# A step of the second layer's experts in another order: next gate products, this pair's outputs, next transposes, then the branch

## Chip, cores, metric

The kernel runs on one core of a Trainium2 chip. The metric is the device time of one execution, in microseconds; the number that counts is the median of three runs. The profile below is of one further execution, and its own time stands beside the median in the table.

## What is computed

Two layers of a backbone over 512 latent tokens of width 1024. Each layer is a mixer followed by a channel mixer of 32 experts; each token goes to two of them. All arithmetic that matters here is float32. The expert part of the reference, which both layers end with:

```python
def hier_moe(h, ...):                # h: 512 tokens x 1024
    ...                              # top-1 group of 4, then top-2 of its 8 experts
    for e in range(N_EXPERTS):       # 32
        he = (silu(t @ w_gate[e]) * (t @ w_up[e])) @ w_down[e]   # 1024 -> 256 -> 1024
        out = out + dense_w[:, e:e + 1] * he
x = x + g2 * hier_moe(h2, ...)
```

The kernel does not run each expert over all tokens: the routing sorts the tokens by expert, and an expert gets 64 slots (`SLOT`) at once. An expert with more than 64 tokens is run again for the rest, decided on the chip by counts.

## The kernel before

The change concerns `experts` in its second-layer form (`l == 1`, `sent = True`). The experts are taken in 16 pairs, `pair(j)` being the expert numbers `p` and `p + 16`, one pair a step. The functions of a step, with the lines under which the profile lists them:

- `windows(j)` (L493, L496): ScalarE copies the pair's 2 x 64 token columns out of the sorted tokens `m.xs` into `m.xT`. `window(m.xr, ...)` does the same into `m.xr` for the expert that may have a second 64 tokens.
- `gate_up` (L357): 16 float32 matmuls of TensorE (32 records in the trace, two for each) for gate and up of both experts into PSUM bank `pg` (`mps0`). The weights come in four tiles of 1 MB: two hold the input rows of `c` 0 to 3, one for each expert, and two those of `c` 4 to 7, so the first eight matmuls need the first two tiles and the last eight need all four.
- `act` (L362, L363): silu on ScalarE into `m.sg`, times up on VectorE into `m.h`.
- `turn` (L370, L371): two transposes of `m.h` on TensorE into bank `ph` (`mps1`), and ScalarE's copy of them to `m.hT`. In the kernel before, `m.hT` is the memory of `m.sg`, so there is one buffer for transposed rows.
- `down` (L430): 8 float32 matmuls (16 records) with two more 1 MB weight tiles, into banks `py` (`mps2`, `mps3`).
- `once` (L623, L614, L615): VectorE weights the two halves of `py` into `ys`, and GpSimd scatters them by an indirect DMA to `yd`, a table of rows in HBM.
- `more_of` (L451, L452, L453, L370, L371, L459, L631, L615): the whole chain again for one expert of the pair with up to 64 more tokens. It reads the pair's six weight tiles again, and uses `m.sg`, `m.h`, `m.hT` and bank `ph`.
- `first(j + 1, None)`: `gate_up`, `act`, `turn` of the next pair and `windows(j + 2)`.

Which of the two sides of a branch is run (the label `few{l}_{j}`, L669) is decided by the larger count of the pair: with 64 tokens or fewer `few` is run, otherwise the `Else` side, which is laid out directly behind the branch. Every engine that has work in either side branches for itself.

The order around it is that in which the code is written: the whole of `experts` stands in a manual schedule, and each engine runs its instructions in program order. What makes one engine wait for another are semaphores that the framework sets by data and buffers.

The weights are a stream of 96 tiles of 1 MB for the layer (`Stream.emit`, L322 for gate and up, L324 for down, all issued by SyncE). The pool `W` has 13 buffers free for it and one more lies under the tag `more`; 14 tiles are loaded ahead. After that `st.emit(6, j)`, written behind the branch of step `j`, issues the next six tiles into the six buffers of pair `j`, which `more_of` may read as long as the branch is not over. After the 16th pair, `summed` (L653, L657) reads `yd` back in four 1 MB loads and VectorE adds it to the residual `X`; the 16th pair itself goes through another way to `X`, and `done` (L1798) writes the output.

Of the kernel before, what the change touches and what calls it, by code (L numbers as in the profile page):

```python
# [8 lines left out]
F32 = mybir.dt.float32  # L9
# [8 lines left out]
P = 128  # L18
D = 1024
# [97 lines left out]
class Route:  # L117
# [9 lines left out]
    def tile(self, i):  # L127

        k, v, sm = self.k, self.k.nc.vector, self.k.small
        g, e = self.lg[:, i, 0:4], self.lg[:, i, 4:36]  # L130
        mx, er = self.mx, self.er
        r4 = k.rio[:, 28:32]
        t4 = sm.tile([P, 4], F32, name="t4", tag="rt4", bufs=2)
        gr = sm.tile([P, 1], F32, name="gr", tag="rgr", bufs=2)
        t = sm.tile([P, 32], F32, name="t32", tag="rt32", bufs=2)
        em = sm.tile([P, 32], F32, name="em", tag="rem", bufs=2)
        v.tensor_reduce(mx[:, 0, i:i + 1], g, axis=AX.X, op=OP.max)
        v.scalar_tensor_tensor(t4, g, mx[:, 0, i:i + 1], r4, op0=OP.is_ge, op1=OP.mult)
        v.tensor_reduce(gr, t4, axis=AX.X, op=OP.max)
        v.tensor_scalar(t4, r4, gr, -BIG, op0=OP.not_equal, op1=OP.mult)  # L140
        v.tensor_tensor(em.rearrange("p (g x) -> p g x", g=4), e.rearrange("p (g x) -> p g x", g=4),
                        t4[:, :, None].to_broadcast([P, 4, 8]), op=OP.add)
        for c in range(2):
            m, r = mx[:, 1 + c, i:i + 1], er[:, c, i:i + 1]
            v.tensor_reduce(m, em, axis=AX.X, op=OP.max)
            v.scalar_tensor_tensor(t, em, m, k.rio, op0=OP.is_ge, op1=OP.mult)
            v.tensor_reduce(r, t, axis=AX.X, op=OP.max)
            v.tensor_scalar(self.EL[:, c, i], k.rio, r, None, op0=OP.is_equal)
            if c == 0:
                v.scalar_tensor_tensor(em, self.EL[:, 0, i], -BIG, em, op0=OP.mult, op1=OP.add)  # L150
            v.tensor_scalar(self.EL[:, 2 + c, i], k.rio, r, None, op0=OP.is_lt)
        for q in range(2):
            v.tensor_tensor(self.Eb[:, i, 32 * q:32 * q + 32], self.EL[:, 2 * q, i], self.EL[:, 2 * q + 1, i], op=OP.add)
# [141 lines left out]
def pair(j):  # L295

    return 8 * (j % 2) + j // 2
# [55 lines left out]
def gate_up(k, m, st, p, cs):  # L353

    for c in cs:
        for h in range(2):
            k.nc.tensor.matmul(m.pg[64 * h:64 * h + 64, :], m.xT[:, c, 64 * h:64 * h + 64], st.gu(p, h, c), start=(c == 0), stop=(c == 7))  # L357


def act(k, m):  # L360

    k.nc.scalar.activation(m.sg, m.pg[:, 0:256], AF.Silu)  # L362
    k.nc.vector.tensor_tensor(m.h, m.sg, m.pg[:, 256:512], op=OP.mult)  # L363


def turn(k, m, n=P):

    nc = k.nc
    for f in range(2):
        nc.tensor.transpose(m.ph[:, f * P:f * P + n], m.h[0:n, f * P:(f + 1) * P], k.ident[0:n, 0:n])  # L370
    nc.scalar.copy(m.hT[:, :, 0:n], m.ph[:, 0:2 * P].rearrange("p (f s) -> p f s", f=2)[:, :, 0:n])  # L371
# [52 lines left out]
def down(k, m, st, p):  # L424

    nc = k.nc
    for n in range(2):
        for f in range(2):
            for h in range(2):
                nc.tensor.matmul(m.py[n][64 * h:64 * h + 64, :], m.hT[:, f, 64 * h:64 * h + 64],  # L430
                                 st.dn(p, h, f)[:, 512 * n:512 * n + 512], start=(f == 0), stop=(f == 1))
# [43 lines left out]
def experts(k, l, m, st, res, rt, h2d, X, ahead, done):  # L475
# [8 lines left out]
    def ahead_of(label, row, p, most, limit):  # L484

        c = nc.values_load(res.cnt[0:1, row, p:p + 1], engines=(PE,), min_val=0, max_val=most,
                           skip_runtime_bounds_check_because="counts of at most 512 tokens")
        tc.mark_branch_hint_location(label, hint=c > limit, engines=(PE,))

    def window(x, at, act=False):  # L490

        e = mybir.EngineType
        o = nc.values_load(at, engines=(e.Activation if act else e.DVE,), min_val=0, max_val=1024 - SLOT,  # L493
                           skip_runtime_bounds_check_because="starts of at most 960")
        for c in range(4):
            (nc.scalar.copy if act else nc.vector.tensor_copy)(x[:, 2 * c:2 * c + 2], m.xs[c][:, :, bass.ds(o, SLOT)])  # L496

    def windows(j):
        p = pair(j)
        for h in range(2):  # L500
            window(m.xT[:, :, 64 * h:64 * h + 64], res.start[0:1, 0, p + 16 * h:p + 16 * h + 1], True)
# [28 lines left out]
    sent = l == 1  # L530
# [69 lines left out]
    def outs():  # L600
        m.one = Outs(tile([P, 512], "oh"), [tile([P, D], f"y{i}") for i in range(2)])
        m.two = Outs(tile([P, 512], "C0"), [tile([P, D], "S")])
        m.tmp = k.work.tile([P, 512], F32, name="tmp", tag="C1")

    if sent:
        ys = [k.work.tile([P, D], F32, name="ys", tag=f"y{i}") for i in range(2)]
        yx = k.work.tile([P, D], F32, name="yx", tag="S")[:, 0:512]
    else:
        outs()

    def send(n, row, y):

        ix = k.small.tile([P, 1], I32, name="ix", tag="ix", bufs=3)
        nc.vector.tensor_copy(ix, row)  # L614
        nc.gpsimd.indirect_dma_start(out=k.yd[:, :] if n == D else k.yd.rearrange("r (h d) -> (r h) d", h=2), in_=y, in_offset=None,  # L615
                                     out_offset=bass.IndirectOffsetOnAxis(ap=ix, axis=0), bounds_check=1024 * (D // n) - 1, oob_is_err=False)

    def once(j, p):

        y = ys[j % 2]  # L620
        for n in range(2):
            c = slice(512 * n, 512 * n + 512)
            nc.vector.scalar_tensor_tensor(y[:, c], m.py[n], res.w0[:, p:p + 1], m.g2[:, c], op0=OP.mult, op1=OP.mult)  # L623
        send(D, res.tok0[:, p:p + 1], y)
# [9 lines left out]
    def first(j, due):  # L634

        ahead_of(f"few{l}_{j}", 0, pair(j), 512, SLOT)
        gate_up(k, m, st, pair(j), range(8))
        act(k, m)
        if due:
            due.add(k, m, X, (0, 1))  # L640
        turn(k, m)
        if j < 15:
            windows(j + 1)
        if due:
            due.add(k, m, X, (2, 3))
# [13 lines left out]
    for j in range(16):  # L659
        p = pair(j)  # L660
        last = j == 15
        window(m.xr, res.second[0:1, p:p + 1], True)
        ahead_of(f"few{l}_{j}", 0, p, 512, SLOT)
        if j:
            down(k, m, st, p)
        if sent and not last:
            once(j, p)
            few = tc.If(count(0, p, 512) <= SLOT, preferred_fallthrough_block=False, label=f"few{l}_{j}")
            with few as more:  # L669
                first(j + 1, None)  # L670
            with more.Else():
                ahead_of(f"both{l}_{j}", 3, p, 1, 0)
                with tc.If(count(2, p, 3) == 2) as other:
                    more_of(p, 1, res.w[:, 1, p + 16:p + 17], res.tok[:, 1, p + 16:p + 17])
                with other.Else():
                    more_of(p, 0, res.w[:, 1, p:p + 1], res.tok[:, 1, p:p + 1])
                both = tc.If(count(3, p, 1) <= 0, preferred_fallthrough_block=False, label=f"both{l}_{j}")
                with both as rest:
                    pass
                with rest.Else():  # L680
                    with tc.If(count(2, p, 3) == 3):
                        window(m.xr, res.start[0:1, 1, p + 16:p + 17])
                        more_of(p, 1, res.w[:, 1, p + 16:p + 17], res.tok[:, 1, p + 16:p + 17])
                    with tc.If(count(0, p, 512) > 2 * SLOT):
                        with tc.For_i(2, count(1, p, 8), 1) as r:
                            for h in range(2):
                                at = bass.ds(r * 32 + p + 16 * h, 1)
                                for b, t in ((m.ic[:, h:h + 1], res.start), (m.tw[:, h, 0:1], res.w), (m.tw[:, h, 1:2], res.tok)):
                                    nc.vector.tensor_copy(b, t.rearrange("p r e -> p (r e)")[:, at])
                            for h in range(2):  # L690
                                window(m.xr, m.ic[0:1, h:h + 1])
                                more_of(p, h, m.tw[:, h, 0:1], m.tw[:, h, 1:2])
                first(j + 1, None)
            st.emit(6, j)
            continue
        if sent:
            outs()
            summed()
        weighed(k, m, res.w0[:, p:p + 1], res.tok0[:, p:p + 1])
# [1178 lines left out]
```

## Time and profile before

| | us |
|---|---|
| median of three runs (1397.38 to 1403.32) | 1401.59 |
| the profiled execution | 1409.57 |
| span of its instructions | 1407.8 |
| TensorE busy in the span | 1214.5 (86%) |
| VectorE busy | 745.5 (53%) |
| ScalarE busy | 513.8 (36%) |
| mean DMA rate over the span | 242 GB/s |

The second layer's expert steps fill the last fifth, from about 1100 us to 1376 us; behind them is the end of the kernel. Times in all rows are microseconds from the start of the span. TensorE's records appear as PE, its weight loads as PEld, VectorE as DVE, ScalarE as ACT, GpSimd as POOL, SyncE as SP; a q behind an engine means its sequencer. "Idle before" is the engine's gap just ahead of an instruction, with what ended it; "issue" there means that the profile shows nothing that was waited for.

### The profile page before, as it was taken

How to read it: one execution, taken by the hardware profiler on the slowest of the kernel's cores; microseconds unless marked ns; L12 is line 12 of the kernel's file. 1: busy time of each engine (PE TensorE's matmuls, PEld its weight loads, DVE VectorE, ACT ScalarE, POOL GpSimd, SP SyncE). 2: the span in 40 equal slices, each digit the busy share in tenths (PEclk: the TensorE clock that was granted, in tenths of full speed). 3: DMA queues.
4: the chain of work that ended last, by engine and by line, in shares of the span. 5: the costliest groups of instructions: out<-in, count | busy, mean ns of one | idle time of the engine just before them, and what ended most of it. 6: DMA issues, size and time to landing. Idle time of an engine off the chain costs nothing. (4 is left out here: it accounts for less than half of the span.)

```text
span 1407.8 us, 19802 instructions
## 1 busy us (share of the span) xinstructions
PE 1214.5 (86%) x6894; PEld 788.7 (56%) x6894; DVE 745.5 (53%) x1599; ACT 513.8 (36%) x1235; POOL 288.4 (20%) x270
## 2 busy tenths in 40 slices
PE   4998778989987999989979999999995787777875
PEld 2788645445764444444468898997873343333332
DVE  2435788899567545655683455667246411111116
ACT  3444445476444423433351233345224311211111
POOL 0044346586012111111230002220002000000000
PEclk9999989899997999999989999999997999999998
DMA  9411123737656889989766354453367698888883
GB/s 368 157 60 34 74 106 129 297 132 260 268 219 210 328 356 405 421 318 406 327 200 222 117 203 150 147 184 127 144 239 269 244 372 346 344 349 347 326 358 128
DMA packets 59297, 341.11 MB, mean 242 GB/s; under 512 B 9817, under 2 KB 10073, under 8 KB 24370
## 3 DMA queue, kind: packets, MB, share of 16 engines
q1 hardware_dynamic: 50834, 314.68, 57.3%
q0 software_dynamic: 8224, 23.61, 5.1%
q8 instruction: 105, 1.72, 0.5%
q14 instruction: 134, 1.10, 0.2%
HBM read 321.96 MB, written 21.80 MB: 244 GB/s over the span
## 5 line engine op out<-in xcount | busy, mean ns | idle before, releaser
L357 PE MATMUL mps<-w,xT 128*64 128x512 f32 x1024 | 251.9, 643 | 41.5 <-issue 26.7
L357 PEld LDWEIGHTS mps<-w,xT 128*64 128x64 f32 x1024 | 101.9, 148 | 185.8 <-issue 180.9
L806 PE MATMUL ps_c<-wch,hxh 128*128 128x256 f32 x512 | 147.4, 288 | 2.0 <-ACT hxh L812 2.0
L808 PE MATMUL ps_c<-wch,hxl 128*128 128x256 f32 x512 | 145.8, 285 | 1.5 <-DVE rm_m L98 0.9
L807 PE MATMUL ps_c<-wcl,hxh 128*128 128x256 f32 x512 | 146.0, 285 | 0.0
L363 DVE TENSOR_TENSOR mix<-mix,mps 128x256 f32<-128x256 f32 x32 | 13.5, 421 | 234.3 <-ACT mix L362 234.3
L430 PE MATMUL mps<-w,mix 128*64 128x512 f32 x512 | 118.6, 605 | 8.1 <-ACT mix L371 7.2
L362 ACT ACTIVATE mix<-mps 128x256 f32<-128x256 f32 x32 | 12.3, 384 | 275.6 <-PE mps L357 272.8
L997 POOL TENSOR_TENSOR acc<-acc,ctp 128x497 f32<-128x497 f32 (+14 forms) x71 | 103.2, 1481 | 29.6 <-ACT ctp L996 29.6
L806 PEld LDWEIGHTS ps_c<-wch,hxh 128*128 128x128 f32 x512 | 98.9, 193 | 7.8 <-issue 4.2
L808 PEld LDWEIGHTS ps_c<-wch,hxl 128*128 128x128 f32 x512 | 98.8, 193 | 4.5 <-issue 1.7
L807 PEld LDWEIGHTS ps_c<-wcl,hxh 128*128 128x128 f32 x512 | 98.9, 193 | 4.2 <-issue 3.4
L411 POOL TENSOR_TENSOR X<-X,tmp 128x512 f32<-128x512 f32 x32 | 41.2, 1287 | 204.7 <-ACT tmp L410 181.4
L400 PE MATMUL mps<-oy,ooh 128*128 128x512 f32 x272 | 74.8, 416 | 1.9 <-ACTq L729 1.7
L430 PEld LDWEIGHTS mps<-w,mix 128*64 128x64 f32 x512 | 35.4, 138 | 72.5 <-issue 55.5
L413 DVE TENSOR_TENSOR X<-X,mps 128x512 f32<-128x512 f32 x101 | 64.6, 683 | 5.4 <-PE mps L400 4.3
L806 PE MATMUL ps_o<-woh,yTh 128*128 128x512 f32 x160 | 63.8, 401 | 2.9 <-DVE res L1541 1.7
L400 PEld LDWEIGHTS mps<-oy,ooh 128*128 128x128 f32 x272 | 49.9, 193 | 25.5 <-issue 11.7
L807 PE MATMUL ps_o<-wol,yTh 128*128 128x512 f32 x160 | 63.5, 397 | 0.0
L808 PE MATMUL ps_o<-woh,yTl 128*128 128x512 f32 x160 | 62.9, 394 | 0.0
L812 POOL TENSOR_TENSOR vs<-v,vs 128x512 fp32r<-128x512 f32 x16 | 23.0, 1440 | 182.1 <-ACT vs L812 174.7
L991 DVE SCALAR_TENSOR_TENSOR acc<-z,cl,acc 128x508 f32<-128x508 f32 (+14 forms) x49 | 58.9, 1225 | 0.0
(430 smaller groups left out, 2389.8 us busy)
## 6 DMA issues: line engine op xcount, KB each, us to landing
w<-in_w_gu_dram SPq DMA_DIRECT2D x128, 1024.0 KB
w<-in_w_down_dram SPq DMA_DIRECT2D x64, 1024.0 KB
wada<-in_w_ada_dram SPq DMA_DIRECT2D x48, 1024.0 KB
wc<-in_c_w_in_dram SPq DMA_DIRECT2D x16, 1024.0 KB
wo<-in_c_w_out_dram SPq DMA_DIRECT2D x8, 1024.0 KB
X<-in_x_dram SPq DMA_DIRECT2D x4, 1024.0 KB
wo<-in_ab_w_out_dram SPq DMA_DIRECT2D x4, 1024.0 KB
yd<-zero SPq DMA_DIRECT2D x4, 1024.0 KB
```

Of the source, the lines that this page charges most:

```text
L357: k.nc.tensor.matmul(m.pg[64 * h:64 * h + 64, :], m.xT[:, c, 64 * h:64 * h + 64], st.gu(p, h, c), start=(c == 0), stop=(c == 7))
L363: k.nc.vector.tensor_tensor(m.h, m.sg, m.pg[:, 256:512], op=OP.mult)
L400: k.nc.tensor.matmul(po, self.oh[:, i * P:i * P + P], y[:, 512 * n:512 * n + 512], start=start and y is self.y[0], stop=stop and y is self ...
L411: k.nc.gpsimd.tensor_tensor(X[i][:, c], X[i][:, c], m.tmp, op=OP.add)
L413: k.nc.vector.tensor_tensor(X[i][:, c], X[i][:, c], po, op=OP.add)
L430: nc.tensor.matmul(m.py[n][64 * h:64 * h + 64, :], m.hT[:, f, 64 * h:64 * h + 64], st.dn(p, h, f)[:, 512 * n:512 * n + 512], start=(f == 0 ...
L806: k.nc.tensor.matmul(out, lh, rh, start=start, stop=False)
L807: k.nc.tensor.matmul(out, lh, rl, start=False, stop=False)
L808: k.nc.tensor.matmul(out, ll, rh, start=False, stop=stop)
L812: for i in (k.nc.scalar.copy(hi, src), (eng or k.nc.vector).tensor_tensor(lo, src, hi.bitcast(F32), op=OP.subtract)):
L991: pin(nc.vector.scalar_tensor_tensor(d, zz, w, d, op0=OP.mult, op1=OP.add))
L997: nc.gpsimd.tensor_tensor(d, d, tp, op=OP.add)
```

## The change

For the second layer, steps 0 to 14 are written in a new order. Before: outputs of pair `j` (`down`), `once`, then the branch, in both sides of which the next pair's `first(j + 1)` stands. Now: gate and up of pair `j + 1`, `down` of pair `j`, `act` of `j + 1`, `windows(j + 2)`, `turn` of `j + 1`, `once` of `j`, and then the branch, whose `few` side is empty. So that the transposed rows of pair `j` outlive the gate products of pair `j + 1`, there are two buffers: `hTs[0]`, in unused columns of the tile `ys` of tag `S`, for `turn` and `down`, and `hTs[1]`, the old place, for `more_of`. `st.emit(6, j)` stays behind the branch. The first layer's order is the same as before.

```diff
     if sent:
-        yx = k.work.tile([P, D], F32, name="yx", tag="S")[:, 0:512]
+        yx = k.work.tile([P, D], F32, name="ys", tag="S")
+        hTs = [yx[:, 512:768].rearrange("p (f s) -> p f s", f=2), m.hT]
+        yx = yx[:, 0:512]
@@ in the loop over j
         ahead_of(f"few{l}_{j}", 0, p, 512, SLOT)
-        if j:
-            down(k, m, st, p)
         if sent and not last:
+            gate_up(k, m, st, pair(j + 1), range(8))
+            m.hT = hTs[0]
+            if j:
+                down(k, m, st, p)
+            act(k, m)
+            if j < 14:
+                windows(j + 2)
+            turn(k, m)
+            m.hT = hTs[1]
             once(j, p)
             few = tc.If(count(0, p, 512) <= SLOT, preferred_fallthrough_block=False, label=f"few{l}_{j}")
             with few as more:
-                first(j + 1, None)
+                pass
             with more.Else():
...
-                first(j + 1, None)
             st.emit(6, j)
             continue
         if sent:
+            m.hT = hTs[0]
+        if j:
+            down(k, m, st, p)
+        if sent:
+            m.hT = hTs[1]
             outs()
             summed()
```

Three places in the built program. First TensorE around branch 1, the second of the loop. In the kernel before, `few`'s side of branch 0 ends here with the gate products and transposes of pair 1 (L357 and the first L370), and then come `down` of pair 1 and branch 1 (L669):

```order
L357 MATMUL mps_15807<-w,xT 64x512 x16
L370 MATMUL mps_15808<-ct,mix 128x128 x2
L669 UNCONDITIONAL_BRANCH
L486 TENSOR_LOAD cnt
L488 REGISTER_ALU
L1874 BRANCH_PREFETCH_HINT
L430 MATMUL mps_15809<-w,mix 64x512 x4
L430 MATMUL mps_15810<-w,mix 64x512 x4
L479 TENSOR_LOAD cnt
L669 COMPARE_AND_BRANCH
```

In the changed kernel the same step, behind branch 0, has the gate products of pair 2, `down` of pair 1, the transposes of pair 2 and branch 1 (L680):

```order
L695 UNCONDITIONAL_BRANCH
L486 TENSOR_LOAD cnt
L488 REGISTER_ALU
L1889 BRANCH_PREFETCH_HINT
L357 MATMUL mps_15807<-w,xT 64x512 x16
L430 MATMUL mps_15809<-w,ys 64x512 x4
L430 MATMUL mps_15810<-w,ys 64x512 x4
L370 MATMUL mps_15808<-ct,mix 128x128 x2
L479 TENSOR_LOAD cnt
L680 COMPARE_AND_BRANCH
```

The gate products of pair 2 have moved from behind branch 1 to the place right behind branch 0, and the transposes from ahead of `down` to behind it.

Second, SyncE behind branch 0, where `st.emit(6, 0)` issues its six tiles (the numbers behind `w_` tell the tiles apart). In the kernel before:

```order
L678 UNCONDITIONAL_BRANCH
L684 UNCONDITIONAL_BRANCH
L669 UNCONDITIONAL_BRANCH x2
L322 DMA w_16574<-in_w_gu_dram 128x2048
L322 DMA w_16576<-in_w_gu_dram 128x2048
L324 DMA w_16578<-in_w_down_dram 128x2048
```

In the changed kernel the same tiles, under other numbers:

```order
L680 UNCONDITIONAL_BRANCH
L689 UNCONDITIONAL_BRANCH
L695 UNCONDITIONAL_BRANCH
L322 DMA w_16527<-in_w_gu_dram 128x2048
L322 DMA w_16529<-in_w_gu_dram 128x2048
L324 DMA w_16531<-in_w_down_dram 128x2048
```

Nothing moved on SyncE: the six issues stand behind branch 0 in both.

Third, where TensorE reads the first two of these tiles, among the gate products of pair 2, whose other two tiles (`w_15805`, `w_15895`) are the last of the 14 that are loaded ahead. In the kernel before this stands in both sides of branch 1 (L669):

```order
L357 MATMUL mps0_15807<-w_15805,xT_15815 64x512
L357 MATMUL mps0_15807<-w_15895,xT_15815 64x512
L357 MATMUL mps0_15807<-w_16574,xT_15815 64x512
L357 MATMUL mps0_15807<-w_16576,xT_15815 64x512
...
L370 MATMUL mps1_15808<-ct_68,mix_15816 128x128 x2
L669 UNCONDITIONAL_BRANCH
```

In the changed kernel it stands ahead of `down` of pair 1, whose weights are `w_15801` and `w_15803`:

```order
L1889 BRANCH_PREFETCH_HINT
L357 MATMUL mps0_15807<-w_15805,xT_15815 64x512
L357 MATMUL mps0_15807<-w_15895,xT_15815 64x512
...
L357 MATMUL mps0_15807<-w_16527,xT_15815 64x512
L357 MATMUL mps0_15807<-w_16529,xT_15815 64x512
...
L430 MATMUL mps2_15809<-w_15801,ys_16219 64x512
L430 MATMUL mps2_15809<-w_15803,ys_16219 64x512
```

The first read of the batch's tiles has moved from behind branch 1 to behind branch 0, with eight matmuls between branch and read.

## Rows read from the trace of the kernel before

**Rows 1.** Windows of the steps; busy us of PE, PEld, DVE, ACT, POOL, clock, DMA share, GB/s.
```profile
1109.66:1366.61 256.95, 200.53 (x913) 86.14 (x910) 38.16 (x76) 48.77 (x206) 18.58 (x19) 0.95 0.88 352
1126.92:1144.72 17.80, 13.33 (x52) 6.29 (x50) 1.99 (x4) 3.25 (x14) 0.97 (x1) 0.88 0.93 369
1144.72:1164.83 20.11, 17.09 (x89) 8.08 (x85) 2.50 (x6) 3.90 (x16) 0.97 (x1) 0.95 0.83 334
```
**Rows 2.** SyncE's waits from 1000 us on: who waited for what, us, times, longest.
```profile
SPq L322 <- PE mps L357: 119.6, 9, 14.7
SPq L322 <- PEq L678: 73.5, 5, 14.9
```
**Rows 3.** The engines' waits from 1095 us on, the same columns.
```profile
PE mps L357 <- issue: 20.4, 10, 2.9
...
PE mps L370 <- DVE mix L363: 15.6, 15, 1.1
...
PE mps L430 <- ACT mix L371: 7.2, 14, 0.7
PE mps L357 <- PEq L486: 7.1, 5, 2.3
```
**Rows 4.** Windows from two of SyncE's issues (rows 8) on, columns as in rows 1.
```profile
1144.72:1146.90 2.18, 2.18 (x7) 1.16 (x5) 0.00 (x0) 0.00 (x0) 0.00 (x0) 0.50 0.62 132
1146.90:1159.50 12.60, 11.07 (x62) 5.48 (x60) 1.98 (x4) 3.25 (x14) 0.74 (x1) 1.00 1.01 426
...
1164.83:1167.00 2.17, 1.05 (x6) 0.50 (x8) 1.57 (x3) 0.00 (x0) 0.26 (x1) 1.00 0.57 113
1167.00:1171.40 4.40, 4.40 (x24) 1.50 (x21) 0.00 (x0) 0.00 (x0) 0.73 (x1) 1.00 1.00 400
```
**Rows 5.** Timeline of TensorE, steps 2 to 4: start, us, instruction, count, idle before.
```profile
1136.53 3.65 PE L430 MATMUL mps<-w,mix 128*64 128x512 f32 x16 [0.46 <-ACT mix L371]
1143.12 8.88 PE L357 MATMUL mps<-w,xT 128*64 128x512 f32 x32 [2.94 <-issue]
1153.07 0.44 PE L370 MATMUL mps<-ct,mix 128*128 128x128 f32 x2 [1.07 <-DVE mix L363]
1153.97 3.65 PE L430 MATMUL mps<-w,mix 128*64 128x512 f32 x16 [0.46 <-ACT mix L371]
...
1165.95 7.09 PE L357 MATMUL mps<-w,xT 128*64 128x512 f32 x32 [1.25 <-PEq L486]
...
1175.09 3.65 PE L430 MATMUL mps<-w,mix 128*64 128x512 f32 x16 [0.63 <-ACT mix L371]
1180.88 8.88 PE L357 MATMUL mps<-w,xT 128*64 128x512 f32 x32 [2.13 <-issue]
```
**Rows 6.** Timeline from the last steps on, all engines.
```profile
1349.10 7.18 PE L357 MATMUL mps<-w,xT 128*64 128x512 f32 x32 [2.72 <-issue]
...
1358.25 3.65 PE L430 MATMUL mps<-w,mix 128*64 128x512 f32 x16 [0.46 <-ACT mix L371]
...
1363.04 0.97 POOL L615 DMA_INDIRECT yd<-ys,ix  x1 [14.55 <-DVE ix L614]
1364.58 9.39 PE L357 MATMUL mps<-w,xT 128*64 128x512 f32 x32 [2.68 <-issue]
1366.61 2.19 SPq L653 DMA_DIRECT2D yt<-yd  x4
...
1374.91 10.71 DVE L657 TENSOR_TENSOR X<-X,yt 128x512 f32<-128x512 f32 x16
```
**Rows 7.** Line 669, the branch, on TensorE's sequencer: ns min/median/max.
```profile
L669 PEldq COMPARE_BRANCH  x19: 87/481/5350, 1119.8 to 1358.8; - x19
```
**Rows 8.** Timeline of SyncE at one batch: start, from first to last issue, count.
```profile
1164.83 1.09 SPq L322 DMA_DIRECT2D w<-in_w_gu_dram  x2
```
**Rows 9.** Timeline of TensorE where the loop begins.
```profile
1107.70 9.64 PE L357 MATMUL mps<-w,xT 128*64 128x512 f32 x32 [3.73 <-ACT mix L496]
```
**Rows 10.** Timeline of ScalarE there.
```profile
1104.95 1.78 ACT L496 COPY xT<-xs 128x128 f32 x8
```

## The prediction

> **What bounds the kernel now.** Only the second layer's expert steps and what follows them are touched, so I read that stretch. First the windows cut at the moments when SyncE starts a batch of six weight tiles [rows 1]: 14 steps in 256.95 us, a step of 17.8 us where `few` is taken and 20.1 where the `Else` side is. Of steps 0 to 14, five (3, 5, 7, 9, 11) take the `Else` side: the waits count five for its line L678 [rows 2]. In a step TensorE is busy for 13.3 of 17.8 us and the DMAs for 0.93 of the time, so neither is full alone, and one must ask who waits for whom. TensorE's waits [rows 3] are the 15.6 us for the activation, 7.2 us for the copy of the transposes, and 27.5 us at the branch (20.4 + 7.1); no wait for a weight tile stands among them. SyncE in turn waits 193.1 us for TensorE (119.6 + 73.5) before it may refill buffers [rows 2]. So today TensorE's chain with its branch stalls sets the pace, and the weights arrive in time, with little to spare: a batch is 6.3 MB, at 426 GB/s [rows 4] 14.8 us, and 2.2 us pass first at 113 to 132 GB/s; together 17.0 of the 17.8 us.
>
> **What the order does to the weights.** There are buffers for 14 tiles, six for a pair. Batch j goes into the buffers of pair j and is issued when TensorE has left branch j, before and after the change: nothing moves on SyncE. Before, its first two tiles (`w_16574`, `w_16576`) are read behind `down`, activation and branch of the next step, about 17 us later. Now gate and up of pair j + 2 come directly behind branch j, and their last eight matmuls read exactly these two tiles (`w_16527`, `w_16529`). TensorE must now wait in the middle of each `gate_up` for tiles that could not be issued earlier. The wait closes a loop: batch issued, two tiles land, half a `gate_up`, activation, transposes, branch, buffers free, next batch issued. I cost one turn of it.
>
> Issue to landing of the second tile: in the 2.17 us behind an issue the DMAs start 0.25 MB, in the 4.40 us behind that 1.76 MB [rows 4]; 2.1 MB are under way after 6.8 us. The scatter of `once` (0.5 MB), issued at most 2 us earlier in the new order, shares the queue, 1.2 us at 400 GB/s. I take 8.0; ends 6.8 and 9.0 (a start-up twice as long).
>
> Second half of `gate_up`: half of 7.09 is 3.55. Behind idle times of 2 us and more `gate_up` took 8.88 instead of 7.09 [rows 5] since its first part ran at the lower of the two clocks, a granted 0.50 (1.2 of 2.4 GHz) in the window [rows 4]; all of the excess in one half makes 5.33. Another time it took 7.18 behind 2.72 idle [rows 6]. I take 4.6.
>
> By the Trainium skill (TensorE: Matmul & The Clock Gate, section HAM oscillation) a wait for a DMA in each tile makes each tile start at the lower clock. By that rule it would be 5.33 every time, rival C; the rows here show both.
>
> From the end of `gate_up` to the release of the buffers, `few` taken: from the start of `down` to the next `gate_up` it was 6.59, 5.79 and 6.33 us [rows 5, 6], of which up to 5.35 are the branch instruction itself [rows 7]; since `down` takes 3.65, TensorE's sequencer evidently starts on the branch soon after `down` begins. In the new order the transposes stand between, and wait 1.07 us for the activation [rows 5], which runs beside `down`; the branch starts that much later: 1.07 + 6.3 = 7.4 to the next `gate_up`. The release comes about 1 us ahead of it, as on the `Else` side today (issue at 1164.83, `gate_up` at 1165.95 [rows 5, 8]). So 6.4; ends 5.9 and 6.7. The 1.07 and 0.46 us that TensorE idles for activation and copy are thus gone from TensorE, but `down` then covers a part of the branch stall less.
>
> The same, `Else` taken: `down` to issue was 10.86 us (1153.97 to 1164.83); the transposes come on top (0.44), and the copy out of bank `mps1`, since `more_of` writes that bank (0.46 as for L430): 11.8; ends 11.3 and 12.3.
>
> With 0.1 for the hand-over a turn is 0.1 + 8.0 + 4.6 + 6.4 = 19.1 us (`few`) or 24.5 (`Else`), against 17.8 and 20.1 now. VectorE, ScalarE and GpSimd are busy under 4 us a turn [rows 1], the windows and the copy of ScalarE beside `down`, so none of them ends last.
>
> **The two ends of the loop.** Batch 0 was issued at 1109.66, 1.96 us after `gate_up` of pair 1 started at 1107.70 [rows 9]. Now that `gate_up` comes ahead of branch 0. It can start at about 1106, when ScalarE has copied half of its window [rows 10], ends 9.4 later, and the release follows 6.4 after that: batch 0 at 1121.8, 12.1 us later than before.
>
> From batch 0, thirteen turns (branches 1 to 13: 8 `few`, 5 `Else`) lead to batch 13: 8 x 19.1 + 5 x 24.5 = 275.3, so 1397.1. `gate_up` of pair 15 ends 12.7 later at 1409.8. Before it ended at 1373.97 [rows 6]: 35.8 us later.
>
> The read-back of `yd`: before, pair 14's `down` and scatter ran ahead of this `gate_up`, which hid them: the adds (L657) start 0.94 us behind its end. Now `down` of pair 14 comes behind it: 3.65, then 4.71 until the load is issued (1361.90 to 1366.61), then about 5 until 1 MB is there (8.0 less 2.5 for the second tile, less part of the scatter): the adds start 13.4 behind, 12.4 later than before. What follows is as before.
>
> **Sum.** 35.8 + 12.4 = 48.2 us. The profiled execution would go from 1409.57 to 1457.8. It lay 8.0 us above the median; on the median, 1401.59 + 48.2 = 1449.8, and I say 1449. With all low ends a turn is 16.4 or 21.8, under the 17.0 that the DMAs need for a batch; with 17.0 and 21.8 the sum is about 15 us more than now. With all high ends (21.1, 26.7) it is about 77 more. All terms will not lie at one end, so 1424 to 1475.
>
> **Rivals.**
> B, not slower: the weights do arrive in time, as they would if the pool had buffers free beyond the 14. Then only TensorE's chain counts: 9 `few` turns save 0.9 us (7.4 instead of 1.07 + 0.44 + 0.46 + 6.3), 5 `Else` turns 1.07, and the first `gate_up` starts 1.7 earlier: 15 us, less the 12.4 us at the read-back: 1399, no change. For it: no wait for a tile shows today. Against it: the built order, in which the tile is issued behind the branch and read half a `gate_up` later. It decides where `down` or `gate_up` waits for no tile. 0.06. If the branch stall shrinks too, 9 x 2 less: 1381, faster: 0.03.
>
> C, slower still: the second half runs at the lower clock each time, 13 x 0.73 = 9.5 us more: 1459. For it 8.88 in the rows, against it 7.18. 0.18.
>
> D, less slow: the empty `few` side makes the jump shorter, by one copy of `first`, and the branch no longer stalls. Then the release waits only for the transposes, 4.1 + 0.3 behind `gate_up`: 2.0 x 9 less, 1431. Against it: the `few` jump still passes four copies of `more_of`. 0.10.
> By the Trainium skill (Runtime: NRT & Kernel Launch, section Instruction fetch mechanics) a taken branch stalls if its target is outside the pages that the sequencer holds. The 5.35 us here agree with that; how many pages TensorE holds no row shows.
>
> **How the numbers follow.** The forecast 1449 has 0.63, C 0.18, D 0.10, all slower and in the range, 0.91 together; B 0.06 within 0.5%, which is about what a measurement here can tell from no change; faster 0.03.
>
> **What would show it.** TensorE waits for a DMA of `w` in the middle of L357, some 2 to 4 us in nearly every step, which it never does now; batches 19 and 24 us apart instead of 17.8 and 20.1, with DMA idle between them and a mean rate near 305 GB/s instead of 352; no wait of L370's transposes for VectorE; first batch near 1122; L657 waiting for its loads, 13 us behind the last L357. I am wrong if L357 shows no such wait, or if batches still follow at 17.8 us.

## The result, and the profile after

The changed kernel takes 1438.39 us (median of 1434.85 to 1442.02), the kernel before, timed beside it, 1402.45 (1397.38 to 1407.12): a ratio of 1.0256, 95% interval 1.0222 to 1.0291, or +36 us where +48 was forecast. It is slower, and the wait that was forecast is there; that the size came near is in part luck, since terms were off on both sides.

Executions of one kernel spread by some 20 us here (the kernel before from 1388.16 to 1409.57 in all its runs), so where one profile is set against another I use the **stage**: from the first transposes of the tokens gathered for the second layer's experts (L517) to the end of the span. This row in the kernel before:

```profile
1077.16 1.94 PE L517 MATMUL mps<-ct,rows 128*128 128x128 f32 x8 [2.15 <-DMA rows<-h2d,g]
```

and in the changed one:

```profile
1065.55 1.94 PE L517 MATMUL mps<-ct,rows 128*128 128x128 f32 x8 [2.18 <-DMA rows<-h2d,g]
```

The stage grew from 330.6 us (1407.8 less 1077.16) to 374.7 (1440.2 less 1065.55), by 44.0. The 11.6 us that the changed kernel is early here come from code that both have in common.

Windows of the changed kernel between SyncE's batches, columns as in [rows 1]: batch 0 to 13, one `few` turn, one `Else` turn. A turn is the time from one batch to the next; turn j crosses branch j.

```profile
1103.51:1375.32 271.81, 207.21 (x860) 79.08 (x860) 36.22 (x73) 47.23 (x195) 17.70 (x18) 0.94 0.80 316
1119.74:1136.75 17.01, 13.11 (x50) 4.35 (x50) 1.98 (x5) 3.35 (x15) 0.99 (x1) 1.00 1.00 398
1136.75:1164.80 28.05, 21.90 (x92) 7.78 (x92) 2.86 (x8) 4.28 (x17) 1.95 (x2) 0.88 0.66 253
```

13 turns take 271.8 us instead of 240.5: on the mean 17.2 (`few`) and 26.9 (`Else`) instead of 17.6 and 19.9. The sum compares as it stands, the split does not: in the kernel before a batch is issued 1.1 to 2.0 us behind the start of `gate_up` where `few` was taken and 1.1 ahead of it where `Else` was, in the changed kernel always 1.2 to 1.4 ahead. From the start of one `gate_up` to the start of the next, the kernel before takes 16.0 and 22.7 us and the changed one 17.2 and 26.9. So the five `Else` turns carry 21 us of the loss, the eight `few` turns 9. In a `few` turn the DMAs are busy for 0.82 to 1.00 of the time, in an `Else` turn for two thirds of it: there all six tiles have landed, and none may be issued until the next branch is over.

Waits of TensorE from 1095 us on, columns as in [rows 2]:

```profile
PE mps L357 <- DMA w<-in_w_gu_dram: 37.4, 25, 2.6
PE mps L357 <- PEq L486: 19.2, 12, 4.4
```

and of SyncE:

```profile
SPq L322 <- PEq L680: 118.8, 9, 18.7
SPq L322 <- PEq L689: 104.9, 5, 22.0
...
SPq L656 <- DMA yd<-ys,ix: 18.2, 2, 18.0
```

The first row is new: [rows 3] have no wait for a tile of `w` at all. The 15.6 us for the activation in [rows 3] are gone. Where the new wait sits, in TensorE's timeline of the third turn:

```profile
1136.19 0.44 PE L370 MATMUL mps<-ct,mix 128*128 128x128 f32 x2
1137.93 4.71 PE L357 MATMUL mps<-w,xT 128*64 128x512 f32 x16 [1.30 <-PEq L486]
1143.28 1.07 PE L357 MATMUL mps<-w,xT 128*64 128x512 f32 x2 [0.64 <-DMA w<-in_w_gu_dram]
1146.70 5.99 PE L357 MATMUL mps<-w,xT 128*64 128x512 f32 x13 [2.35 <-DMA w<-in_w_gu_dram]
...
1152.54 4.01 PE L430 MATMUL mps<-w,ys 128*64 128x512 f32 x15
1156.48 0.44 PE L370 MATMUL mps<-ct,mix 128*128 128x128 f32 x2
1157.38 3.67 PE L451 MATMUL mps<-w,mix 128*64 128x256 f32 x32 [0.46 <-ACT ys L371]
```

The batch was issued at 1136.75. Sixteen records of `gate_up` run, two more once the first tile of the batch is there, and the rest waits for the second. Such a pause stands in every step from pair 2 on. In [rows 5] the same 32 records are one piece.

The branch, L680 and its `Else` counterpart L689, on TensorE's sequencer (ns, minimum, median, maximum):

```profile
L680 PEldq COMPARE_BRANCH  x25: 82/195/1707, 1103.0 to 1393.4; - x25
```

```profile
L689 PEldq COMPARE_BRANCH  x10: 186/278/3865, 1163.4 to 1337.7; - x10
```

The stalls of up to 5350 ns in [rows 7] are gone from the `few` branch. The end of the changed kernel:

```profile
1388.68 0.59 PE L357 MATMUL mps<-w,xT 128*64 128x512 f32 x1
...
1393.83 0.98 POOL L618 DMA_INDIRECT yd<-ys,ix  x1 [16.90 <-DVE ix L617]
...
1396.61 2.90 SPq L656 DMA_DIRECT2D yt<-yd  x4
...
1401.46 2.75 DVE L660 TENSOR_TENSOR X<-X,yt 128x512 f32<-128x512 f32 x4 [7.91 <-DMA yt<-yd]
1406.18 8.06 DVE L660 TENSOR_TENSOR X<-X,yt 128x512 f32<-128x512 f32 x12 [1.97 <-DMA yt<-yd]
```

The adds start 12.2 us behind the last `gate_up` (1389.27), where [rows 6] have 0.94, and now wait twice for their loads.

### The profile page after: what moved, and what is told of

It is laid out like the page before. It is cut to its first block, busy times and chain, and to the rows that moved or that the text cites. A ratio compares the mean times of both kernels' runs of the same rounds, so it can differ in the third digit from the quotient of the medians.

```text
span 1440.2 us, 19875 instructions
## 1 busy us (share of the span) xinstructions
PE 1225.1 (85%) x6894; PEld 782.0 (54%) x6894; DVE 743.9 (52%) x1599; ACT 515.6 (36%) x1235; POOL 288.8 (20%) x270
## 4 chain that ended last, share of the span: by engine, by line
PE 20%; issue 13%; DMA 11%; DVE 5%; POOL 1%; ACT 1%; POOLq 0%; DVEq 0%; SPq 0%; ACTq 0%
DMA yd<-ys,ix 9%; PE ps_c L823 4%; PE ps_c L821 4%; PE ps_c L822 4%; PE ps_o L821 2%; PE ps_o L823 2%; PE ps_o L822 2%; PE ps_ada L841 1%; DMA yt<-yd 1%; POOL vs L827 1%; DVE X L660 1%; PE ps_l L114 0%; DMA wc<-in_c_w_in_dram 0%; PE mps L400 0%; DVE v L1465 0%
## 5 line engine op out<-in xcount | busy, mean ns | idle before, releaser
L357 PE MATMUL mps<-w,xT 128*64 128x512 f32 x1024 | 273.0, 643 | 70.7 <-DMA w<-in_w_gu_dram 37.4
L357 PEld LDWEIGHTS mps<-w,xT 128*64 128x64 f32 x1024 | 95.9, 147 | 235.3 <-issue 180.6
L362 ACT ACTIVATE mix<-mps 128x256 f32<-128x256 f32 x32 | 12.3, 385 | 264.7 <-issue 164.5
L400 PE MATMUL mps<-oy,ooh 128*128 128x512 f32 x272 | 76.3, 423 | 12.7 <-DVE mps L419 10.9
L618 POOL DMA_INDIRECT yd<-ys,ix x20 | 19.6, 982 | 286.5 <-DVE ix L617 215.5
L400 PEld LDWEIGHTS mps<-oy,ooh 128*128 128x128 f32 x272 | 50.4, 196 | 36.8 <-issue 11.7
L430 PE MATMUL mps<-w,ys 128*64 128x512 f32 x240 | 66.2, 595 | 1.3 <-PEq L486 1.3
L430 PE MATMUL mps<-w,mix 128*64 128x512 f32 x272 | 62.1, 598 | 0.0
```

Of the source, the lines that this page charges most:

```text
L400: k.nc.tensor.matmul(po, self.oh[:, i * P:i * P + P], y[:, 512 * n:512 * n + 512], start=start and y is self.y[0], stop=stop and y is self ...
```

## The experiments

Theory: the loop of the prediction (batch issued, second tile lands, half a `gate_up`, `down`, branch, next batch). Rivals: the time is lost at branches, in a longer `Else` side, or by the clock. All ratios are to the kernel before. Turns are counted between batch issues in the profiled execution (in ahead_10 between the fifth tiles of the batches). Since the issue stands elsewhere in the old order, the columns `few` and `Else` compare within the new order only; the column of 13 turns compares throughout.

| kernel | ratio (95%) | `few` | `Else` | 13 turns | stage |
|---|---|---|---|---|---|
| before | | 17.6 | 19.9 | 240.5 | 330.6 |
| changed | 1.0256 (1.0222 to 1.0291) | 17.2 | 26.9 | 271.8 | 374.7 |
| down_first | 1.0799 (1.0717 to 1.0881) | 22.7 | 31.2 | 338.0 | 446.7 |
| early_tiles | 1.0153 (1.0090 to 1.0216) | 14.3 | 27.0 | 249.6 | 347.9 |
| gu_first | 1.0063 (1.0033 to 1.0094) | 14.7 | 23.8 | 236.4 | 343.4 |
| half_behind | 1.0235 (1.0167 to 1.0302) | 16.6 | 27.5 | 270.2 | 369.0 |
| last_old | 1.0201 (1.0128 to 1.0275) | 17.2 | 25.9 | 267.3 | 364.4 |
| late_hint | 1.0346 (1.0272 to 1.0420) | 18.7 | 24.7 | 273.5 | 371.9 |
| short_branch | 1.0021 (0.9986 to 1.0055) | 15.9 | 22.8 | 240.6 | 333.4 |
| early_hint | 1.0020 (0.9991 to 1.0049) | 17.5 | 19.5 | 237.5 | 328.5 |
| short_early | 1.0027 (0.9998 to 1.0055) | 16.2 | 22.7 | 243.4 | 333.4 |
| ahead_10 | 1.0027 (0.9999 to 1.0055) | 16.9 | 19.4 | 232.5 | 326.1 |
| no_load_old | 0.9751 (0.9711 to 0.9791) | | | | 296.6 |
| no_load_new | 0.9764 (0.9721 to 0.9806) | | | | 296.5 |

**Make the tile later: down_first.**

```diff
+            q = self.n
+            if l and q >= 14:
+                q += (2, 2, -2, -2, 0, 0)[(q - 14) % 6]
-            p, j = divmod(self.n, 6)
+            p, j = divmod(q, 6)
```

> The changed kernel with the order inside a batch turned: the two tiles for down ahead of the two for the second half of the next gate_up, which thus land two tiles (2.1 MB, 5.0 us at 420 GB/s) later. Loop theory: the pause in gate_up grows by 5.0 us in each of 13 turns, few turns 22, Else turns 32, the time 1438 + 65 = 1503 (1485 to 1510). Rival (the time is lost at branches or by the clock): no change, 1438.

1514.94 us, 5 us above the range. The 13 turns grew by 66.2 us, with 65 expected. TensorE's timeline of turn 1, whose batch was issued at 1131.06 (`gate_up` is L360, `down` L433 here):

```profile
1132.29 3.75 PE L360 MATMUL mps<-w,xT 128*64 128x512 f32 x16 [1.35 <-PEq L489]
1142.17 1.97 PE L360 MATMUL mps<-w,xT 128*64 128x512 f32 x2 [6.13 <-DMA w<-in_w_gu_dram]
1144.71 3.77 PE L360 MATMUL mps<-w,xT 128*64 128x512 f32 x13 [0.56 <-DMA w<-in_w_gu_dram]
```

The pause follows the tile, and every turn with it: TensorE's waits for `w` grew from 37.4 to 89.4 us. The clock adds to it: the second half of `gate_up` had a granted 0.59 to 0.72 in all 14 steps, where the changed kernel had 1.00 in eight. The loop is real; a loss at branches or by the clock alone would not follow the tile.

**Take the wait away: early_tiles.**

```diff
-def gate_up(k, m, st, p, cs):
+def gate_up(k, m, st, p, cs, cut=8):
...
-            k.nc.tensor.matmul(m.pg[64 * h:64 * h + 64, :], m.xT[:, c, 64 * h:64 * h + 64], st.gu(p, h, c), start=(c == 0), stop=(c == 7))
+            k.nc.tensor.matmul(m.pg[64 * h:64 * h + 64, :], m.xT[:, c, 64 * h:64 * h + 64], st.gu(p, h, c % cut), start=(c == 0), stop=(c == 7))
...
-            gate_up(k, m, st, pair(j + 1), range(8))
+            gate_up(k, m, st, pair(j + 1), range(8), 4)
```

> The changed kernel, but the last eight matmuls of the moved gate_up read the same two weight tiles as the first eight, so the gate products of the second layer's pairs 1 to 15 are made with half of the weights twice; all 96 tiles are still loaded. Loop theory (gate_up waits for tiles that are issued only behind the branch ahead of it): the pause in the middle of gate_up is gone; a turn is then 1.2 + 7.1 + 3.9 = 12.2 us on TensorE where few is taken, under what the DMAs need for a batch, so 15 to 17 us by the DMAs, and 1.2 + 7.1 + 12.8 = 21.1 where Else is taken, against 17.2 and 26.9 in the changed kernel. 13 turns 8 x 16 + 5 x 21.1 = 233.5 instead of 271.8: about 1400 us instead of 1438. Rival, the longer Else side is longer by its own branch and copies: Else turns stay above 25 us and the time above 1430.

1424.04 us, 24 above the forecast and below the rival's 1430: 13 turns 22.2 us shorter, stage 26.8. The `few` turns did what the loop says (14.3, several 12.3). The `Else` turns did not shorten, as the rival has it, but not by its reason. TensorE, from a `few` turn (issues at 1163.76 and 1176.10) into the `Else` turn behind it:

```profile
1164.98 7.19 PE L357 MATMUL mps<-w,xT 128*64 128x512 f32 x32 [1.35 <-PEq L486]
...
1180.44 1.87 PE L357 MATMUL mps<-w,xT 128*64 128x512 f32 x2 [4.46 <-DMA w<-in_w_gu_dram]
1183.21 8.68 PE L357 MATMUL mps<-w,xT 128*64 128x512 f32 x29 [0.91 <-DMA w<-in_w_gu_dram]
...
1196.58 3.67 PE L451 MATMUL mps<-w,mix 128*64 128x256 f32 x32 [0.46 <-ACT ys L371]
```

After a turn of 12.3 us, `gate_up` needs the last two tiles of the batch before, issued 16.7 us earlier, and these are not there. What the `few` turn gains on the weights, the next turn pays. My 21.1 for `Else` had left this out: the first half of `gate_up` hangs on the stream too, one batch later.

**Order the stream as TensorE reads it: gu_first.**

```diff
+            q = self.n
+            if l:
+                q = q + 2 * (10 <= q) if q < 14 else 6 * ((q - 14) // 6) + (10, 11, 18, 19, 20, 21)[(q - 14) % 6]
...
+            if l and self.n > 14:
+                t = self.at[i - (1 if j > 3 else 3), j]
```

> The changed kernel with the stream in the order in which TensorE now reads it: ahead are the six tiles of pair 0 and all four gate and up tiles of pairs 1 and 2; a batch is the two down tiles of pair j + 1 and then the four gate and up tiles of pair j + 3. Same computation, same 14 buffers. Loop theory: gate_up finds its tiles, the down tiles land while gate_up runs; few turns 15 to 17 us by the DMAs, Else turns 21 to 22; 13 turns 8 x 16 + 5 x 21.3 = 234.5 instead of 271.8, about 1401 us (1392 to 1412). Rival: 1438 as the changed kernel, with Else turns above 25.

1411.64 us, 13 turns 236.4: both as expected, `Else` 2.5 longer than that. Its waits of TensorE (`down` is L438, `gate_up` L365):

```profile
PE mps L438 <- DMA w<-in_w_down_dram: 13.9, 8, 5.7
...
PE mps L365 <- DMA w<-in_w_gu_dram: 2.8, 3, 1.6
```

37.4 us of waits became 16.7, with the same 14 buffers and the same computation. The 13 turns are 4.1 us shorter than in the kernel before, yet the kernel is not faster: outside them batch 0 comes 5.5 us later in the stage, and what follows batch 13 takes 11.4 longer.

**Fill the pause: half_behind.**

```diff
-            gate_up(k, m, st, pair(j + 1), range(8))
+            gate_up(k, m, st, pair(j + 1), range(4))
...
                 down(k, m, st, p)
+            gate_up(k, m, st, pair(j + 1), range(4, 8))
```

> The changed kernel with the second half of gate_up (its last eight matmuls) behind down of this pair instead of ahead of it. Loop theory: down's 3.65 us fill the pause; the wait for the second tile (8.9 us behind the issue) falls from about 2 us to 0.5, and down no longer stands between second half and release, though the activation now does: few 8.9 + 3.6 + 2.0 = 14.5, so 15 to 17 by the DMAs, Else 8.9 + 3.6 + 10.5 = 23; 13 turns 8 x 16 + 5 x 23 = 243 instead of 271.8, about 1410 (1400 to 1420). Rival (time lost at branches or in Else): 1438 or more.

1433.06 us: the forecast of 1410 failed. TensorE's waits for `w` fell from 37.4 to 10.8 us, but the activation came out of `down`'s cover again (14.6 us for it, 15 times), and the `Else` turns (27.5) are no shorter, with `gate_up`'s first tiles up to 2.3 us late behind short `few` turns as in early_tiles.

**The read-back: last_old.**

```diff
-            gate_up(k, m, st, pair(j + 1), range(8))
+            if j < 14:
+                ahead()
...
             st.emit(6, j)
+            if j == 14:
+                ahead()
+                rest_of()
```

(`ahead` is `gate_up` of the next pair, `rest_of` its `act`, `windows` and `turn`.)

> The changed kernel, but step 14 in the old order: down of pair 14, once, the branch, and then gate_up, act and turn of pair 15. Theory: the read-back of yd lies open in the changed kernel since the scatter of pair 14 comes behind gate_up of pair 15; here that gate_up hides it again, 12 us less: 1426 (1421 to 1429). Rival: the read-back waits for something else (the queue behind the last weight tiles): no change, 1438.

1434.70 us, above the range of 1421 to 1429. The ratio fell by 0.55%, 8 us, but the two intervals overlap, so the times alone do not show a gain. In the profile the part behind the last `gate_up` fell from 50.9 to 40.3 us:

```profile
1390.70 9.05 PE L357 MATMUL mps<-w,xT 128*64 128x512 f32 x32 [4.92 <-PEq L690]
1392.64 0.97 POOL L618 DMA_INDIRECT yd<-ys,ix  x1 [10.07 <-DMA yd<-ys,ix]
1397.26 2.24 SPq L656 DMA_DIRECT2D yt<-yd  x4
1402.14 5.41 DVE L660 TENSOR_TENSOR X<-X,yt 128x512 f32<-128x512 f32 x8 [1.45 <-DMA yt<-yd]
```

The adds start 2.4 behind it instead of 12.2, which is what the theory says and not the rival. The scatter was itself held up by the one before it (10.07), which I had not counted.

**No weights at all: no_load_new, no_load_old.** Both kernels with

```diff
+            if l and self.n > 14:
+                self.t[p, j] = self.t[0, j]
+                continue
```

> The changed kernel without the 82 weight tiles that the second layer loads behind its first 14: from pair 2's second half on, all steps read the tiles of the first pair again, so the second layer's products are made with wrong weights and 86 MB are not loaded. What is left is TensorE's own chain in the new order. Loop theory: few turns 12.3 us, Else turns 20 (as the undisturbed ones in early_tiles), 13 turns 8 x 12.3 + 5 x 20 = 198 instead of 271.8: about 1365 us. Rival (the Else side itself is longer in the new order): Else turns stay near 25, above 1385.

> The kernel before without the same 82 weight tiles, wrong in the same way. If TensorE's chain with its branch stalls of 4.4 us and more sets the pace of the kernel before: few turns stay at 17.6 us, Else at 19.9, no change from 1402. If the stalls are long only because the instructions are fetched beside the weights: few turns about 14.5, 13 turns 8 x 14.5 + 5 x 19.9 = 215.5 instead of 240.5, 1377. Either way longer than the 198 of the new order without loads.

1368.56 and 1367.82 us. The new order: 12.2 and 19.8 between two `down`s, as expected, so the `Else` side itself is not longer in the new order (`gate_up` L360, `down` L433):

```profile
1175.55 3.61 PE L433 MATMUL mps<-w,ys 128*64 128x512 f32 x16
...
1195.39 3.61 PE L433 MATMUL mps<-w,ys 128*64 128x512 f32 x16
1198.93 0.44 PE L373 MATMUL mps<-ct,mix 128*128 128x128 f32 x2
1200.65 7.09 PE L360 MATMUL mps<-w,xT 128*64 128x512 f32 x32 [1.28 <-PEq L489]
1207.56 3.61 PE L433 MATMUL mps<-w,ys 128*64 128x512 f32 x16
```

The old order, 12.5 and 21.0. Its `few` turns (12.8 on the mean) are shorter than in either of my cases, its `Else` turns 1 us longer, and the time is below both:

```profile
1173.43 3.65 PE L433 MATMUL mps<-w,mix 128*64 128x512 f32 x16 [0.46 <-ACT mix L374]
...
1194.41 3.65 PE L433 MATMUL mps<-w,mix 128*64 128x512 f32 x16 [0.54 <-ACT mix L374]
1197.89 7.04 PE L360 MATMUL mps<-w,xT 128*64 128x512 f32 x32
...
1206.90 3.65 PE L433 MATMUL mps<-w,mix 128*64 128x512 f32 x16 [0.46 <-ACT mix L374]
```

So without the loads the new order wins nothing on the whole: the last `gate_up` ends 14.5 us earlier in the stage (247.0 against 261.5), and the end takes it back, 10.8 us of it in the open read-back (adds 12.3 behind that `gate_up` instead of 1.5). The loads cost the old order 35 us and the new one 70. The old order's 35 come without any wait for a tile: with the loads the branch takes 4.4 to 5.35 us instead of 1.96 to 3.03, and `gate_up` behind that idle time 8.88 instead of 7.04.

**How many tiles ahead: ahead_10.**

```diff
-        st.emit(NPRE - st.n)
+        st.emit((10 if l else NPRE) - st.n)
```

(and the 14th tile's own issue, `st.emit(1, -1)`, is left to the first layer.)

> The kernel before with 10 tiles loaded ahead in the second layer instead of 14: at a branch four tiles are loaded and not yet read, as in the changed kernel, where eight are in the kernel before. A batch is then down of pair j + 1 and gate and up of pair j + 2. Theory A, the time from the issue to the first read decides: down comes about 8.5 us behind the issue and its tiles land at 8.9, so waits of 0 to 2 us, 13 turns 1 us longer each: 1402 + 13 = 1415 (1405 to 1425). Theory B, the number of tiles ahead decides: as slow as the changed kernel, 1438.

1407.64 us, no wait for a tile anywhere. But the run does not do what I had expected of it. SyncE waits for TensorE only where no buffer is free, and with ten tiles ahead four are: it issues three tiles of a batch as soon as it has passed its own branch, and the other three (from 1131.08 on here) wait for TensorE's:

```profile
1116.35 0.94 SPq L324 DMA_DIRECT2D w<-in_w_down_dram  x2
1117.40 15.42 SPq L322 DMA_DIRECT2D w<-in_w_gu_dram  x4
```

The two `down` tiles of a batch are read 21.5 to 27.8 us behind their issue, not 8.5, and from pair 3 on no tile is read less than 15.8 us behind it; in the kernel before the shortest is 17.9. So neither theory was tested: the run shows only that these 2 us less cost nothing that can be told. A distance of about 8 us stands in gu_first: its `down` tiles are wanted 8 us behind their issue, and TensorE waited for them eight times, 13.9 us. In the new order the first tiles are wanted 5 us behind it (1.2 until `gate_up` starts and half of it).

**The branch stall: short_branch, early_hint, short_early (old order), late_hint (new order).**

```diff
             with few as more:
-                first(j + 1, None)
+                pass
...
-                first(j + 1, None)
+            first(j + 1, None)
             st.emit(6, j)
```

(short_branch. early_hint leaves out the loop's `ahead_of(...)` for `j` above 0; short_early does both; late_hint puts `ahead_of(...)` of the changed kernel behind its `gate_up`.)

> The kernel before, but few's side of the branch is empty and first(j + 1) stands once, behind the branch, instead of in both sides. If the branch stall comes from the long few side (the jump over copies of first): the branch instruction takes under 2 us instead of 4.4 to 5.35 where few is taken, few turns fall from 17.6 us to the 15 to 17 that the DMAs need, time 1402 - 9 x 1.5 = 1388 (1380 to 1395). If the stall ended in the changed kernel because the hint stands a whole gate_up ahead of the branch: the stalls stay at 4.4 to 5.35, time 1402.

> The kernel before with only the first of its two hints for each branch from step 1 on, the one ahead of gate_up; the one ahead of down is left out. If the early hint ends the stalls: branch instructions under 2 us, few turns 15 to 17 instead of 17.6, 1388. If the empty side does: no change, stalls of 4.4 to 5.35, 1402.

> The kernel before with an empty few side, first(j + 1) once behind the branch, and from step 1 on only the hint ahead of gate_up: the two things that the changed kernel does to its branch, in the old order. The branch instruction should take under 2 us in nearly all few turns (it took 0.36 to 0.37 or 5.07 to 5.57 with the empty side alone). If TensorE's chain sets the pace: few turns 14.1, Else 21.5, 13 turns 220, 1402 - 20 = 1382. If the weights do once the stalls are gone: 13 turns stay at 235 to 241 as with the empty side alone, 1400.

> The changed kernel with the prefetch hint for the branch moved from ahead of gate_up to behind it, just ahead of down, where the kernel before has it. If the empty few side ended the stalls: no change, branch instructions under 2 us, 1438. If the early hint did: 4.4 us and more again, the release of the buffers 2 to 2.5 us later in 9 turns, 1438 + 20 = 1458.

1403.53, 1401.52, 1407.69 and 1446.66 us: the three in the old order change nothing that can be told. TensorE's branch instruction where `few` is taken, step 0 aside: early_hint 4.55 to 4.92 us throughout; short_branch 0.36 to 0.37 in four steps, 5.07 to 5.57 in four and 3.47 in the last; short_early 4.51 to 4.88 but for one of 0.39 and a last one of 3.29; late_hint 4.77 to 6.81 in five, less in four; the changed kernel at most 1.71. So neither the empty side, nor the early hint, nor both together explain why the stall is gone: short_early has both and stalls. The row of short_early:

```profile
L670 PEldq COMPARE_BRANCH  x25: 82/197/4875, 1101.8 to 1363.0; - x25
```

Nor does the new order by itself: gu_first has it, with the empty side and the early hint, and took 5.97 and 5.88 us in two steps.

What a stalled branch waits for can be read from the DMA trace, which has queues for instructions. Queues of the kernel before from 1110 to 1366 us (packets, MB, share of 16 engines):

```profile
q1 hardware_dynamic: 11808, 85.99, 83.7%
q0 software_dynamic: 2421, 3.61, 3.9%
q8 instruction: 29, 0.48, 0.7%
q14 instruction: 44, 0.36, 0.4%
```

Every packet of q8 has 16 KB. Over all 14 kernels, TensorE's `few` branch took 0.87 us or more 84 times, and each time it ended 1.33 to 1.65 us behind the end of such a packet. Where it took 0.35 to 0.65 us (60 times), the last packet had ended 0.86 us or more ahead of the branch. So the stall is a wait for instructions; that these packets are TensorE's I read from this agreement alone. In the kernel before the packet starts 2.0 to 3.0 us into the branch (step 0 aside), in no_load_old between 0.5 ahead of its start and 0.4 behind it, in the changed kernel 0.7 to 2.8 ahead in eight of nine steps. Why it starts early in one kernel and late in another stays open.

For late_hint I expected 1438 or 1458; it lies between. Its interval overlaps that of the changed kernel, and in its profile the 13 turns grew by only 1.7 us although `few` turns grew by 1.5 each, while TensorE's waits for `w` fell from 37.4 to 28.2. That fits a branch stall that is mostly made up while the tiles are waited for; it is not shown further.

## Why the prediction held, and which terms were off

By the stage of the two profiled executions, +44.0 us, against the forecast of +48.2:

| term | forecast | measured |
|---|---|---|
| batch 0 | +12.1 | +5.5 |
| 13 turns | +34.8 | +31.3 |
| batch 13 to the end of the last `gate_up` | -11.1 | -9.8 |
| from there to the end | +12.4 | +17.1 |

- **The loop** was the step that carried the forecast, and it holds: the wait in L357, its place and its size (2 to 4 us a turn forecast, 37.4 us in 14 steps measured), confirmed by down_first from one side and gu_first from the other. One sign of being wrong came in all the same: in the `few` turns batches follow at 17.2 us and not at 19.
- **A turn** was mis-sized in both forms, 17.2 instead of 19.1 (`few`) and 26.9 instead of 24.5 (`Else`). Over 13 turns that is 15 us too much and 12 too little; that the sum comes near is luck. From issue to the second half of `gate_up`: 8.1 forecast, 8.9 (`few`) and 9.6 (`Else`) measured. Ahead of an `Else` turn the batch is issued 16 to 17 us behind the last, while the DMAs are still busy with that one, and I had priced it on idle DMAs. The 1.2 us for the scatter on the weights' queue have no row behind them: in the queues above the 86 MB of q1 are the 82 weight tiles, and the 19 scatters have q0, with 0.19 MB each on the mean and not 0.5. Second half: 4.6 forecast, 4.4 and 4.7 measured. Release: `few` 6.4 forecast, 3.9 measured in each of the eight, below rival D's price of 4.4, since the branch does not stall; `Else` 11.8 forecast, 12.6 measured, 11.7 in three of five and more in the two where L689 took 3.87 and 2.70 us.
- **Rival D** gave the mechanism of an absent stall a chance of 0.10, and it happened beside the loop. Its reason, the empty side, does not do it by itself (short_branch, short_early). By the Trainium skill (Runtime: NRT & Kernel Launch, section Instruction fetch mechanics) a taken branch waits for a fetch of its target where that is not among the pages held; the trace agrees, since each stall ends behind a 16 KB packet of an instruction queue. That the same branch takes 1.96 to 3.03 us without the weight loads and 4.4 to 5.35 with them agrees with a fetch that shares the DMAs.
- **Rival C**, the lower clock each time: the second half took 3.62 us in 8 of 14 steps and 5.10 to 6.60 in six. Windows of the halves of turns 1 and 2, granted clock in the third column from the right:

```profile
1129.21:1132.83 3.62, 3.62 (x18) 1.57 (x20) 0.00 (x0) 0.00 (x0) 0.00 (x0) 1.00 1.02 432
1146.70:1153.12 6.42, 6.42 (x18) 2.19 (x20) 0.00 (x0) 0.00 (x0) 0.00 (x0) 0.56 1.01 422
```

  The pauses ahead of them were 2.03 and 2.35 us long. By the Trainium skill (TensorE: Matmul & The Clock Gate, section HAM oscillation) a wait for a DMA in each tile makes the next start slow each time; the waits of that page's kernel are about 3 to 5 us. Here, with pauses of 1.4 to 2.7 us, it was six of 14; in down_first, with 4.0 to 6.5, it was all 14, which agrees. The 4.6 taken between the two ends was near the mean of 4.6.
- **Batch 0** was mis-sized by a step of mine: I added the release of a full turn (6.4) behind `gate_up` of pair 1, but `down` of pair 0 runs ahead of the loop. Only activation, transposes and branch follow, and the batch goes out 1.8 us behind it. The other 2 us are a `gate_up` of 7.95 instead of 9.4 that starts 0.7 earlier in the stage:

```profile
1093.71 7.95 PE L357 MATMUL mps<-w,xT 128*64 128x512 f32 x32 [1.35 <-ACT xT L496]
1102.59 0.44 PE L370 MATMUL mps<-ct,mix 128*128 128x128 f32 x2 [0.93 <-DVE mix L363]
```

```profile
1103.51 1.96 SPq L322 DMA_DIRECT2D w<-in_w_gu_dram  x2
```

- **The read-back**: adds 12.2 behind the last `gate_up`, 13.4 forecast. But "what follows is as before" failed by 5.9 us: the adds wait 1.97 once more for the second load, and the last 3.8 lie behind them, in TensorE's and VectorE's work on pair 15's rest. Of these, 2.8 are two groups of matmuls (L400, 4.08 and 2.93 us instead of 2.55 and 1.67): TensorE had idled 10.94 us until the late adds let VectorE go on, and ran them at a granted 0.50 where it had 1.00 before.
- **Rival B** has the right total for TensorE's chain: 15 us gained and 12.4 lost at the read-back forecast, 14.5 and 10.8 in no_load_old and no_load_new, and the two kernels level. Its parts are not shown: from one `down` to the next a `few` turn gains 0.3 us there and not 0.9, with shorter branch stalls than it reckoned with. It failed at its condition, that the tiles be there.
- "Today TensorE's chain with its branch stalls sets the pace" holds: no kernel in the old order waits for a tile. That taking the stall away would be worth 10 us and more there, as I expected of short_branch, could not be seen in its time: 4 of its 9 `few` turns ran without the stall, and the time did not change. From one `down` to the next these four take 14.0 to 14.1 us where the kernel before takes 14.9 to 17.2, 9 us less together; the four stalled ones among the 13 turns take 17.7 to 19.1 where it takes 15.3 to 17.4, 8 us more, with `gate_up` now behind the join.
- Left over: the stage grew by 44.0 us and the medians by 36.0. One profile of each does not tell whether that is spread.

No kernel here that computes the whole layer beats the one before; the nearest, early_hint, is level with it.

## What to carry to other kernels

When work is moved ahead, follow its inputs back to the release that lets them be loaded: what counts is the time between the issue of a refill and its first read, and not how many buffers there are. With the same 14 buffers, tiles read 18 us and more behind their issue were never waited for, those wanted after 8 us cost 13.9 us of waits (gu_first), and those wanted after 5 us most of 37.4. If the read order changes, change the load order with it; that alone got back most of the loss here. And price a loop of loads on the DMAs as they are in the loop, with the last batch still under way, since a short turn's gain is a debt to the next one.

## What was not expected of the hardware

- The same branch of the same program took 4.4 to 5.35 us on TensorE's sequencer while 1 MB tiles were streaming, and 1.96 to 3.03 with these loads left out. Where `gate_up` behind it had taken 8.88 us, it took 7.04.
- Two kernels with the same empty side and the hint ahead of `gate_up` in both differ in the branch stall, 4.5 us and more (short_early) against at most 1.71 (the changed kernel). In every one of 84 cases the stall ended 1.33 to 1.65 us behind a 16 KB packet of instructions; no run here tells what sets the start of that packet.
- Two pauses of about the same length (2.03 and 2.35 us) left TensorE at a granted 1.00 in one case and 0.56 in the other.
